# Stored weight sums and two more seven-product pairs in a down projection

## The chip, the cores and the metric

The kernel runs on one core of one Trainium2 chip. The metric is the device time of one execution in microseconds (us); lower is better. The core has a matrix engine (TensorE, PE), a vector engine (VectorE, DVE), a scalar engine (ScalarE, ACT), GpSimd (POOL), and SyncE (SP). Each runs its own instructions in order and waits on semaphores for the others. SP and POOL issue most DMAs, each on a queue of its own.

## The reference

One layer of an encoder for 256 positions of width 2048: a mixer block and a convolutional gated MLP, then a final norm. The change touches the MLP alone:

```python
def conv_ffn(x, g_norm, w_up, conv_k, conv_b, w_down):
    h = rms_norm(x, g_norm)
    up = h @ w_up                       # 256 x 2048 @ 2048 x 11008
    ...                                 # depthwise conv of width 3 over positions
    gate, val = jnp.split(up, 2, axis=-1)
    return x + (jax.nn.silu(gate) * val) @ w_down    # 256 x 5504 @ 5504 x 2048
```

The mixer block before it (an input projection, a gated branch, neighbourhood attention, an output projection) is as in the kernel before.

## The kernel before

All weights are float32. For the matrix engine each float32 operand is written as a sum of two values of a shorter format, a high part and a low part; one product then is three matmuls (a *triple*: high x high, low x high, high x low). ACT makes the high part by a copy (`whi`, L151), DVE the low part by a subtraction (`wlo`, L152). The notes call the two together the split.

Weights arrive in *pieces* by DMAs on SP into five buffers (`wraw`, `LOAD_AHEAD`). For the down projection a piece is 128 rows of `w_down` by 1024 columns, 512 KB. `begin(i)` is called ahead of the matmuls of piece i: it issues loads up to piece i + 4, splits up to piece i + 3 (four buffers each of `whi` and `wlo`), and then runs the tasks that were registered for step i with `at(i, ...)`. So the order on every engine is written out by these step numbers.

The down projection is two *groups* of 1024 columns, one after the other; each walks over the 43 blocks of 128 rows, taken two at a time as *pairs* (21 pairs and one single block). With two blocks of positions, two of rows and two of columns, a pair is a 2 x 2 by 2 x 2 block product. Done plainly it is eight triples (`plain`), twelve matmuls a piece. In the pairs listed in `DOWN_QUADS` it is done with seven products in the manner of Strassen and Winograd: the products take sums of the activations' blocks and of the weights' blocks, and the results are put together after the last such pair of a group (`ev_sums`). At the first piece of such a pair three triples are issued, at the second four.

For a seven-product pair whose first piece is step i:

- The sums of the activations (`sums` in `ev_up`) are made and split during the up projection, stored to device memory (`so`, L1010), and fetched in each group at step i - 4 by a POOL DMA (`stored`, L1157) into one of two tiles (`s0`, `s1`).
- The four sums of weight blocks (`weight_sums`, L324 to L327) are made by DVE at step i - 3 from both pieces' buffers, into the tiles `t13` and `t24`, of which there is one each.
- They are split at step i - 2 (`weight_sums_split`, L334 on ACT and L335 on DVE) into `h13`, `h24`, `l13`, `l24`, of which there are two sets (`both_rooms`).
- Of the pieces themselves only one half of the first and both halves of the second are split (`units`).

The up projection ahead of it runs over 22 groups (`g_up`) of eight pieces of `w_up`, with the convolution and the gate of one group (`conv`, `gate`) as tasks of the next one's steps. The convolution of the last groups runs in the first steps of the down projection. At step 6 of the down projection `open_fin` has POOL load two parts of the final norm's scale (`gfin`).

Of the kernel before, what the change touches and what calls it, by code (L numbers as in the profile page):

```python
# [8 lines left out]
F32 = mybir.dt.float32  # L9
# [46 lines left out]
OUT_ORDER = (tuple(range(16)), (0, 1, 6, 7, 2, 3, 10, 11, 4, 5, 8, 9, 12, 13, 14, 15))  # L56
TURN_X2 = (13, 1)
Y_GAP = 224
DOWN_PAIRS = (3, 5, 7, 9, 10, 12, 14, 16, 17, 19)
DOWN_QUADS = (DOWN_PAIRS, (2, 4, 6, 8, 9, 11, 13, 14, 16, 18))  # L60


@with_exitstack
def trunk_kernel(ctx, tc, x, x_t, vecs, w_in, ln_g, ln_b, w_st, b_s, rpb, w_branch, w_out, w_up, w_down,
                 norm_final, out):
    nc = tc.nc
    ctx.enter_context(tc.manual_schedule())

    def pool(name, side="left", bufs=1, space=None):
        kw = {} if space is None else {"space": space}  # L70
        st = ExitStack()
        p = st.enter_context(tc.tile_pool(name=name, bufs=bufs, side=side, reuse_waits="tile", **kw))
        return p, st

    def keep(name, side="left", bufs=1, space=None):
        p, st = pool(name, side, bufs, space)
        ctx.push(st)
        return p
# [22 lines left out]
    def plan_wide(src, row0, order, c0):  # L101
        first = len(pieces)
        for k in order:
            pieces.append((src, row0 + k * 128, 2, (c0, 512, 1, 0), 512))
        return first

    raw, split_t = {}, {}
    whole, units = {}, {}
    n_loaded = [0]
    n_split = [0]  # L110

    def load_to(n):
        while n_loaded[0] < min(n, len(pieces)):
            i = n_loaded[0]
            n_loaded[0] += 1
            if i in preload:
                for f in preload[i]:
                    f()
            src, r0, kn, (c0, cn, nb, cs), step = pieces[i]
            w = wpool.tile([128, 2, 512], F32, name="wraw", bufs=LOAD_AHEAD)  # L120
            ld = src.shape[-1]
            if i == 0:
                for k in range(kn):
                    nc.sync.dma_start(w[:, k, :cn], src[r0:r0 + 128, c0 + k * step:c0 + k * step + cn])
            elif nb == 1:
                nc.sync.dma_start(
                    w[:, :kn, :cn],
                    bass.AP(tensor=src.tensor, offset=src.offset + r0 * ld + c0,
                            ap=[[ld, 128], [step, kn], [1, cn]]))
            else:  # L130
                for b in range(nb):
                    nc.sync.dma_start(
                        w[:, :kn, b * cn:(b + 1) * cn],
                        bass.AP(tensor=src.tensor, offset=src.offset + r0 * ld + c0 + b * cs,
                                ap=[[ld, 128], [step, kn], [1, cn]]))
            raw[i] = w
            if i in whole:
                whole[i] = w
# [31 lines left out]
    def at(i, f):  # L170
        tasks.setdefault(i, []).append(f)
# [6 lines left out]
    def begin(i):  # L178
        cur[0] = i
        load_to(i + LOAD_AHEAD)  # L180
        if i < len(SPLIT_TO):
            run_tasks(i)
            split_to(SPLIT_TO[i])
        else:
            split_to(i + SPLIT_AHEAD + 1)
            run_tasks(i)
# [75 lines left out]

    def wide(src, row0, order, c0, acts, quads, room, done, sums=None, odd=None, stored=None, split_room=None):
        n0 = plan_wide(src, row0, order, c0)
        boxes = {}
        for n, q in enumerate(quads):
            i = n0 + 2 * q
            own = odd if odd and n % 2 else split_room or room  # L270
            whole[i] = whole[i + 1] = None
            units[i], units[i + 1] = 1, 2
            b = boxes[q] = {}
            if stored:
                b["acts"] = {}
                at(i - 4, lambda b=b, k=order[2 * q]: stored(k // 2, b["acts"]))
            else:
                b["acts"] = sums[order[2 * q]]
            at(i - 3, lambda i=i, b=b: weight_sums(i, b, room))
            at(i - 2, lambda b=b, own=own: weight_sums_split(b, own))  # L280
        return ("wide", n0, order, acts, quads, boxes, done)

# [38 lines left out]
    def weight_sums(i, box, room):  # L321
        r0, r1 = whole.pop(i), whole.pop(i + 1)
        t13, t24 = room("t13", F32), room("t24", F32)
        nc.vector.tensor_add(t13[:, 0], r0[:, 0], r0[:, 1])  # L324
        nc.vector.tensor_add(t24[:, 1], t13[:, 0], r1[:, 1])
        nc.vector.tensor_add(t13[:, 1], r0[:, 1], r1[:, 1])  # L326
        nc.vector.tensor_add(t24[:, 0], r1[:, 0], t24[:, 1])  # L327
        box["w"] = (t13, t24)

    def weight_sums_split(box, room):  # L330
        u = []
        for name, t in zip(("13", "24"), box.pop("w")):
            h, l = room("h" + name, F32R), room("l" + name, F32R)
            nc.scalar.activation(h, t, AF.Copy)  # L334
            nc.vector.tensor_sub(l, t, h.bitcast(F32))  # L335
            u.append((h, l))
        box["t"] = {1: [x[:, 0] for x in u[0]], 3: [x[:, 1] for x in u[0]],
                    2: [x[:, 1] for x in u[1]], 4: [x[:, 0] for x in u[1]]}
# [166 lines left out]
    def first_room(name, dt):  # L505
        return ypool.tile([128, 2, 512], dt, name=f"y{first_rooms.index('t13' if name == 'f' else name)}")
# [387 lines left out]
    def ev_sums(j, room):  # L894
        def done(P, i):
            x2 = rs["x2"]
            p1, p5, p6, p7 = P
            x11, x12, x21, x22 = (x2[:, t, c * 512:(c + 1) * 512] for t in range(2) for c in (j, j + 1))
            m = {}

            def first_half():
                ab, cd = room("t13", F32), room("t24", F32)
                m["v"], m["u3"], m["w"] = cd[:, 0], cd[:, 1], ab[:, 0]
                nc.scalar.activation(ab[:, 0], p1, AF.Copy)
                nc.vector.tensor_add(x11, p1, x11)
                nc.vector.tensor_sub(ab[:, 1], ab[:, 0], p6)
                nc.vector.tensor_add(m["v"], p5, ab[:, 1])
                nc.vector.tensor_add(m["u3"], p7, ab[:, 1])
                nc.vector.tensor_add(m["w"], p5, m["u3"])

            def second_half():
                nc.vector.tensor_sub(x12, x12, m["v"])
                nc.vector.tensor_add(x21, x21, m["u3"])
                nc.vector.tensor_sub(x22, x22, m["w"])

            at(i + 1, first_half)
            at(i + 2, second_half)
        return done
# [47 lines left out]
    ff = {}  # L966
# [132 lines left out]
    w_br, w_o, w_u, w_d = w_branch[0], w_out[0], w_up[0], w_down[0]  # L1099
# [6 lines left out]
    def odd_room(name, dt):  # L1106
        return s_room["odd"].tile([128, 2, 512], dt, name=name)

    first_sums = {2 * q: {} for q, _, _ in X_SUMS}
    g_v = wide(w_in2, 0, V_ORDER, V0, xt, V_QUADS, first_room, (ev_v_sums, ev_v), first_sums,  # L1110
               odd_room)
    g_va = wide(w_in2, 0, VA_ORDER, VA0, xt, VA_QUADS, first_room, (ev_va_sums, ev_va), first_sums)
    for n, (q, i, j) in enumerate(X_SUMS):
        sum_acts_at(i, j, first_sums[2 * q], lambda q=q: q,
                    lambda name, dt, i=i: first_room("s2" if name == "f" and i < 9 else name, dt), f"s{n}", True)
# [19 lines left out]
    for n, q in enumerate(GATE_PAIRS):  # L1135
        i = g_gw[0][1] - 3 + 3 * n
        sum_acts_at(i, i + 1, x_sums[2 * q], lambda q=q: x_pairs[q], sums_room, f"s{n}")
    for n, q in enumerate(OUT_PAIRS):
        i = g_o[0][1] + 3 + 3 * n
        sum_acts_at(i, i + 1, m_sums[2 * q], lambda q=q: mg["pairs"][q], sums_room, f"s{n}")  # L1140
    g_up = []
# [12 lines left out]
    def stored(pair, box):  # L1154
        n = ff["turn"] = ff.get("turn", -1) + 1
        o = down_room(f"s{n % 2}", F32R)
        nc.gpsimd.dma_start(o.bitcast(F32), ff["kept"][pair])  # L1157
        box["s"] = sums_of(o)

    def down_order(g):  # L1160
        free = [p for p in range(NF // 2) if p not in DOWN_PAIRS]
        kept = list(DOWN_PAIRS)
        pairs = [(kept if q in DOWN_QUADS[g] else free).pop(0) for q in range(NF // 2)]
        return tuple(2 * p + kk for p in pairs for kk in range(2)) + (NF - 1,)

    g_dn = [wide(w_d, 0, down_order(g), g * 1024, lambda k: ff["a"][k], DOWN_QUADS[g], down_room,
                 (ev_sums(2 * g, down_room), ev_down if g == 0 else finish), stored=stored, split_room=both_rooms) for g in range(2)]
    dram = keep("dram", space=bass.MemoryType.DRAM)
    ff["kept"] = {p: dram.tile([128, 2, 512], F32, name=f"sums{p}") for p in DOWN_PAIRS}

    preload[0] = [lambda: load_xt(0, 1)]
# [170 lines left out]
```

## Time and profile before

| | |
|---|---|
| median of 3 runs | 1307.95 us (1307.38 to 1308.11) |
| profiled execution | 1307.83 us, its span 1306.0 us |
| granted clock of TensorE, mean | 0.997 |
| PE, DVE, ACT, POOL busy | 99%, 82%, 59%, 8% of the span |
| DMA | 277.19 MB, mean 212 GB/s |
| up projection | about 590 to 1076 us |
| down projection, first matmul to last | 1076.3 to 1297.0 us |

The span is the time from the first to the last instruction of the profiled execution; the device time has a little around it. In the page, a row of 40 digits shows the busy share of each fortieth of the span in tenths. A row such as `wlo<-wraw,whi` names the tile written and the tiles read, L152 the line of the kernel. In the order of time the columns are start, duration, engine and line; in square brackets is how long the engine was idle before and what ended that. Durations of successive instructions of one engine overlap a little, so the pace is read from start to start.

### The profile page before, as it was taken

What the parts mean: (1) busy time and instruction counts of PE and PEld (TensorE: products, weight loads), DVE (VectorE), ACT (ScalarE), POOL (GpSimd) and SP (SyncE); (2) the same over time, 40 slices, a digit from 0 to 9 for tenths busy, and PEclk for the clock granted to TensorE, in tenths of its full rate; (3) what the DMA queues carried; (4) which work ended last, traced back from release to release, by engine and by line L of the source; (5) the groups of instructions that cost most, each with busy time, mean ns of one, the idle gap of its engine ahead of it and who ended that gap; (6) DMA issues with size and microseconds to landing.
All of it is one profiled execution on the core that took longest, in us unless ns stands there. A gap on an engine that the chain in (4) does not pass through costs nothing.

```text
span 1306.0 us, 19254 instructions
## 1 busy us (share of the span) xinstructions
PE 1293.6 (99%) x6712; PEld 1103.9 (85%) x6712; DVE 1072.5 (82%) x1616; ACT 776.8 (59%) x1153; POOL 104.7 (8%) x206
## 2 busy tenths in 40 slices
PE   9999999999999999999999999999999999999997
PEld 7888888888888888888888888888888888888885
DVE  7997777667689966986778878787888889999997
ACT  7766476666655644556556556565555656665563
POOL 0005405413000000000000000000000000000000
PEclk9999999999999999999999999999999999999998
DMA  9779657556556657565566566666666658876782
GB/s 351 251 243 258 191 166 214 175 171 195 177 170 204 218 182 248 202 211 163 177 195 209 182 211 198 215 194 212 191 211 199 215 161 286 288 267 227 265 290 105
DMA packets 174225, 277.19 MB, mean 212 GB/s; under 512 B 13488, under 2 KB 121904, under 8 KB 174128
## 3 DMA queue, kind: packets, MB, share of 16 engines
q1 hardware_dynamic: 165520, 252.28, 59.5%
q0 software_dynamic: 8032, 23.03, 5.5%
q8 instruction: 52, 0.85, 0.3%
q10 hardware_dynamic: 576, 0.66, 0.1%
q14 instruction: 45, 0.37, 0.1%
HBM read 266.48 MB, written 7.34 MB: 210 GB/s over the span
## 4 chain that ended last, share of the span: by engine, by line
PE 96%; DVE 1%; ACT 1%; DMA 1%; issue 0%; SPq 0%; ACTq 0%; DVEq 0%
PE bank L203 31%; PE bank L207 16%; PE bank L291 11%; PE bank L289 11%; PE bank L290 11%; PE bank L231 5%; PE bank L233 4%; PE bank L232 4%; DMA wraw<-in_w_in_dram 1%; PE bank L756 1%; PE bank L806 0%; DVE wlo L152 0%; PE bank L622 0%; PE bank L796 0%; PE bank L887 0%
## 5 line engine op out<-in xcount | busy, mean ns | idle before, releaser
L152 DVE TENSOR_TENSOR wlo<-wraw,whi 128x1024 fp32r<-128x1024 f32 (+1 forms) x472 | 546.0, 1170 | 182.5 <-ACT whi L151 100.4
L151 ACT ACTIVATE whi<-wraw 128x1024 fp32r<-128x1024 f32 (+1 forms) x472 | 470.3, 1010 | 218.4 <-PE bank L290 85.1
L203 PE MATMUL bank<-h,whi 128*128 128x512 f32 x1760 | 425.5, 392 | 0.0
L203 PEld LDWEIGHTS bank<-h,whi 128*128 128x128 f32 x1760 | 322.1, 188 | 61.7
L207 PEld LDWEIGHTS bank<-h,wlo 128*128 128x128 f32 x1760 | 225.9, 191 | 8.8
L207 PE MATMUL bank<-h,wlo 128*128 128x256 f32 x1760 | 228.6, 283 | 0.0
L985 ACT ACTIVATE tc<-ta,ck 128x256 f32<-128x256 f32 x86 | 47.1, 594 | 117.1 <-DVE ta L983 117.1
L291 PE MATMUL bank<-wlo,a 128*128 128x512 f32 x224 | 87.3, 390 | 0.0
L290 PE MATMUL bank<-whi,a 128*128 128x512 f32 x224 | 87.2, 389 | 0.0
L289 PE MATMUL bank<-whi,a 128*128 128x512 f32 x224 | 87.1, 389 | 0.0
L289 PE MATMUL bank<-whi,h 128*128 128x512 f32 x210 | 82.4, 393 | 0.6 <-ACT h L495 0.6
L291 PE MATMUL bank<-wlo,h 128*128 128x512 f32 x210 | 81.9, 390 | 0.7 <-DVE wlo L152 0.7
L290 PE MATMUL bank<-whi,h 128*128 128x512 f32 x210 | 81.8, 390 | 0.8 <-DVE h L496 0.8
L334 ACT ACTIVATE h<-h 128x1024 fp32r<-128x1024 f32 x40 | 40.2, 1053 | 33.7 <-DVE h L326 33.7
L988 DVE SCALAR_TENSOR_TENSOR tc<-ta,ck,tc 128x255 f32<-128x255 f32 x86 | 41.4, 481 | 14.4 <-ACT tc L985 14.4
L231 PE MATMUL bank<-whi,y 128*128 128x512 f32 x128 | 50.5, 394 | 0.0
L231 PE MATMUL bank<-whi,h 128*128 128x512 f32 x128 | 50.4, 394 | 0.0
L233 PE MATMUL bank<-wlo,h 128*128 128x512 f32 x128 | 49.9, 390 | 0.0
L233 PE MATMUL bank<-wlo,y 128*128 128x512 f32 x128 | 49.9, 390 | 0.0
L232 PE MATMUL bank<-whi,y 128*128 128x512 f32 x128 | 49.8, 389 | 0.0
L232 PE MATMUL bank<-whi,h 128*128 128x512 f32 x128 | 49.8, 389 | 0.0
L291 PEld LDWEIGHTS bank<-wlo,a 128*128 128x128 f32 x224 | 42.0, 188 | 9.1 <-DVE wlo L152 0.3
(284 smaller groups left out, 1786.0 us busy)
## 6 DMA issues: line engine op xcount, KB each, us to landing
wraw<-in_w_up_dram SPq DMA_DIRECT2D x336, 256.0 KB, 3.2
wraw<-in_w_in_dram SPq DMA_DIRECT2D x111, 512.0 KB, 4.5
wraw<-in_w_down_dram SPq DMA_DIRECT2D x86, 512.0 KB, 5.4
wraw<-in_w_in_dram SPq DMA_DIRECT2D x66, 256.0 KB, 3.3
wraw<-in_w_branch_dram SPq DMA_DIRECT2D x32, 512.0 KB, 4.6
wraw<-in_w_out_dram SPq DMA_DIRECT2D x32, 512.0 KB, 4.0
h<-sums POOLq DMA_DIRECT2D x20, 512.0 KB, 7.0
sums<-so POOLq DMA_DIRECT2D x10, 512.0 KB, 5.4
```

Of the source, the lines that this page charges most:

```text
L151: nc.scalar.activation(h[:, k, :m], w[:, k, :m], AF.Copy)
L152: nc.vector.tensor_sub(l[:, k, :m], w[:, k, :m], h[:, k, :m].bitcast(F32))
L203: nc.tensor.matmul(p, h[:, k - k0, b * 128:(b + 1) * 128], acts(k), start=k == 0, stop=k == nk - 1)
L207: nc.tensor.matmul(p[:, :T], l[:, k - k0, b * 128:(b + 1) * 128], acts(k)[:, 0, :], start=False, stop=False)
L231: nc.tensor.matmul(p, xh, h[:, kk, :m], start=st, stop=False)
L232: nc.tensor.matmul(p, xl, h[:, kk, :m], start=False, stop=False)
L233: nc.tensor.matmul(p, xh, l[:, kk, :m], start=False, stop=sp)
L289: nc.tensor.matmul(p, xh, h, start=st, stop=False)
L290: nc.tensor.matmul(p, xl, h, start=False, stop=False)
L291: nc.tensor.matmul(p, xh, l, start=False, stop=sp)
L985: nc.scalar.activation(v, u, AF.Identity, scale=ck[:, 1, ch:ch + 1], bias=ck[:, 3, ch:ch + 1])
L988: nc.vector.scalar_tensor_tensor(v[:, 1:], u[:, :T - 1], ck[:, 0, ch:ch + 1], v[:, 1:], op0=OP.mult, op1=OP.add)
```

## The change

There are now twelve seven-product pairs in each group instead of ten, and they stand in adjacent twos: 3 and 4, 6 and 7, and so on in the first group, 2 and 3, 5 and 6 and so on in the second. For four of the twelve in each group (`DOWN_KEPT`, the first of each of the middle four twos) the four weight sums are made ahead:

- During the up projection, in groups 3, 5, ... 17, `sums_ahead` loads a pair's weights (1 MB) on POOL's queue at a group's first step, makes the four sums on DVE at its steps 4 and 5, and stores them to device memory (1 MB) on POOL's queue.
- In the down projection `stored_weights` fetches them with two POOL DMAs of 512 KB into `t13` and `t24` at step i - 6. `weight_sums` is left out for these pairs; `weight_sums_split` at step i - 2 is as before.
- The first piece of such a pair is loaded by half, since only its first 512 columns are needed (`halved`).
- Two more pairs' activation sums are made and stored.

```diff
-DOWN_PAIRS = (3, 5, 7, 9, 10, 12, 14, 16, 17, 19)
-DOWN_QUADS = (DOWN_PAIRS, (2, 4, 6, 8, 9, 11, 13, 14, 16, 18))
+DOWN_PAIRS = (3, 4, 6, 7, 9, 10, 12, 13, 15, 16, 18, 19)
+DOWN_QUADS = (DOWN_PAIRS, (2, 3, 5, 6, 8, 9, 11, 12, 14, 15, 17, 18))
+DOWN_KEPT = ((6, 9, 12, 15), (5, 8, 11, 14))
...
             src, r0, kn, (c0, cn, nb, cs), step = pieces[i]
+            if i in halved:
+                kn = 1
...
-            whole[i] = whole[i + 1] = None
             units[i], units[i + 1] = 1, 2
+            if q in kept:
+                halved.add(i)
+            else:
+                whole[i] = whole[i + 1] = None
...
-            at(i - 3, lambda i=i, b=b: weight_sums(i, b, room))
+            if q in kept:
+                at(i - 6, lambda b=b, k=order[2 * q]: stored_weights(c0, k // 2, b, room))
+            else:
+                at(i - 3, lambda i=i, b=b: weight_sums(i, b, room))
             at(i - 2, lambda b=b, own=own: weight_sums_split(b, own))
...
+    def stored_weights(c0, pair, box, room):
+        box["w"] = room("t13", F32), room("t24", F32)
+        for n, t in enumerate(box["w"]):
+            nc.gpsimd.dma_start(t, ff["weights"][c0, pair][:, 2 * n:2 * n + 2])
+
+    def sums_ahead(src, c0, pair, i):
+        box = {}
+
+        def load():
+            w = box["w"] = ff["more"].tile([128, 4, 512], F32, name="tw")
+            ld = src.shape[-1]
+            nc.gpsimd.dma_start(w, bass.AP(tensor=src.tensor, offset=src.offset + 256 * pair * ld + c0,
+                                           ap=[[ld, 128], [128 * ld, 2], [512, 2], [1, 512]]))
+
+        def first_two():
+            w = box["w"]
+            nc.vector.tensor_add(w[:, 0], w[:, 0], w[:, 1])
+            nc.vector.tensor_add(w[:, 1], w[:, 1], w[:, 3])
+
+        def last_two():
+            w = box["w"]
+            nc.vector.tensor_add(w[:, 3], w[:, 0], w[:, 3])
+            nc.vector.tensor_add(w[:, 2], w[:, 2], w[:, 3])
+            nc.gpsimd.dma_start(ff["weights"][c0, pair], w)
+
+        at(i, load)
+        at(i + 4, first_two)
+        at(i + 5, last_two)
...
+    jobs = [(g * 1024, down_order(g)[2 * q] // 2) for g in range(2) for q in DOWN_KEPT[g]]
+    ff["weights"] = {job: dram.tile([128, 4, 512], F32, name=f"weights{n}") for n, job in enumerate(jobs)}
+    for n, job in enumerate(jobs):
+        sums_ahead(w_d, *job, g_up[3 + 2 * n][1])
```

More of the change, by code (lines that the diff above doesn't have):

```diff
@@ L107, in trunk_kernel @@
     raw, split_t = {}, {}
-    whole, units = {}, {}
+    whole, units, halved = {}, {}, set()
     n_loaded = [0]
@@ L260, in run_group, with wide @@
             done(ps, b)
-    def wide(src, row0, order, c0, acts, quads, room, done, sums=None, odd=None, stored=None, split_room=None):
+    def wide(src, row0, order, c0, acts, quads, room, done, sums=None, odd=None, stored=None, split_room=None, kept=()):
         n0 = plan_wide(src, row0, order, c0)
@@ L1166, in trunk_kernel @@
     g_dn = [wide(w_d, 0, down_order(g), g * 1024, lambda k: ff["a"][k], DOWN_QUADS[g], down_room,
-                 (ev_sums(2 * g, down_room), ev_down if g == 0 else finish), stored=stored, split_room=both_rooms) for g in range(2)]
+                 (ev_sums(2 * g, down_room), ev_down if g == 0 else finish), stored=stored, split_room=both_rooms, kept=DOWN_KEPT[g]) for g in range(2)]
     dram = keep("dram", space=bass.MemoryType.DRAM)
+    jobs = [(g * 1024, down_order(g)[2 * q] // 2) for g in range(2) for q in DOWN_KEPT[g]]
+    ff["weights"] = {job: dram.tile([128, 4, 512], F32, name=f"weights{n}") for n, job in enumerate(jobs)}
+    for n, job in enumerate(jobs):
+        sums_ahead(w_d, *job, g_up[3 + 2 * n][1])
     ff["kept"] = {p: dram.tile([128, 2, 512], F32, name=f"sums{p}") for p in DOWN_PAIRS}
```

## The prediction

> **What bounds the kernel now.** I read the page from the top: engine shares, the 40 slices, the chain; then windows of the stage that the change touches, and inside it the order of time on each engine.
>
> ```profile
> PE 1293.6 (99%) x6712; PEld 1103.9 (85%) x6712; DVE 1072.5 (82%) x1616; ACT 776.8 (59%) x1153; POOL 104.7 (8%) x206
> ...
> DVE  7997777667689966986778878787888889999997
> ...
> DMA  9779657556556657565566566666666658876782
> ...
> PE 96%; DVE 1%; ACT 1%; DMA 1%; issue 0%; SPq 0%; ACTq 0%; DVEq 0%
> ```
>
> TensorE (PE) is busy for 99% and makes 96% of the chain that ends last: the time falls only with the number of products, and rises with every wait that reaches PE. In the last seven slices, the down projection, VectorE (DVE) stands at 9 and the DMA engines at 7 to 8, both higher than before. The windows say it in numbers (first the up projection, then the two groups of the down projection); the columns are busy time of each engine, the granted clock, the DMA share and GB/s:
>
> ```profile
> core 0: us, PE busy (x) PEld busy (x) DVE busy (x) ACT busy (x) POOL busy (x), PEclk, DMA share, GB/s
> 700.00:1000.00 300.00, 300.00 (x1727) 265.20 (x1726) 244.37 (x418) 176.56 (x280) 4.32 (x8) 1.00 0.65 203
> 1080.00:1180.00 100.00, 100.00 (x443) 82.77 (x442) 95.99 (x116) 60.23 (x69) 6.39 (x12) 1.00 0.81 279
> 1200.00:1275.00 75.00, 75.00 (x332) 62.10 (x332) 73.81 (x90) 45.19 (x50) 5.31 (x10) 1.00 0.78 274
> ```
>
> DVE has 19% free in the up projection (244.4 of 300) and 2 to 4% in the down projection. PE is never short there: its one wait for DVE in the whole stage is this, and the loads are held back by buffers that DVE has yet to free, not by the memory:
>
> ```profile
> SPq L126 <- DVE wlo L152: 106.2, 58, 4.8
> ...
> PEld bank L291 <- DVE wlo L152: 0.3, 1, 0.3
> ```
>
> **What the change takes off PE.** A pair done plainly is 8 triples of matmuls, a seven-product pair 7. The groups go from ten such pairs to twelve: 4 triples less, 12 matmuls. Starts of matmuls in order of time (first of the stage, two a triple apart, last):
>
> ```profile
> 1076.31 0.39 PE L289 MATMUL bank<-whi,a 128*128 128x512 f32 x1
> ...
> 1109.83 0.39 PE L289 MATMUL bank<-whi,a 128*128 128x512 f32 x1
> ...
> 1110.51 0.39 PE L289 MATMUL bank<-whi,a 128*128 128x512 f32 x1
> ...
> 1296.63 0.39 PE L291 MATMUL bank<-wlo,a 128*128 128x512 f32 x1
> ```
>
> A triple takes 0.68 us, a matmul 0.227 (the 0.39 is one matmul's pipelined length). The stage has 2 x (10 x 21 + 11 x 24 + 12) = 972 matmuls; (1296.63 - 1076.31) / 971 = 0.2269, so it holds almost no gap. Twelve fewer: **-2.7 us**, 0.21%. That is the whole possible gain. About 0.2% (2.6 us) is what a measurement of this kernel can tell from no change.
>
> **DVE's account.** Its order in time around step 6 of the first group:
>
> ```profile
> 1092.00 1.22 DVE L152 TENSOR_TENSOR wlo<-wraw,whi 128x1024 fp32r<-128x1024 f32 x1
> 1093.13 2.35 DVE L335 TENSOR_TENSOR h<-h,h 128x1024 fp32r<-128x1024 f32 x2
> 1095.40 2.95 DVE L152 TENSOR_TENSOR wlo<-wraw,whi 128x1024 fp32r<-128x1024 f32 x3
> 1098.28 0.68 DVE L324 TENSOR_TENSOR h<-wraw 128x512 f32<-128x512 f32 x1
> ...
> 1100.81 1.22 DVE L152 TENSOR_TENSOR wlo<-wraw,whi 128x1024 fp32r<-128x1024 f32 x1
> 1101.94 2.36 DVE L335 TENSOR_TENSOR h<-h,h 128x1024 fp32r<-128x1024 f32 x2
> ```
>
> From start to start: a full split 1.13, the two splits of a pair's sums 2.27, the three of 1095.40 (two full, one half) 2.88, so a half split 0.62, and the four weight sums 1098.28 to 1100.81, 2.53. A seven-product pair costs DVE 0.62 + 1.13 + 2.53 + 2.27 = 6.55 us against 21 x 0.227 = 4.8 on PE; a plain pair 2.26 against 5.4. A kept pair drops the 2.53. Over the stage 16 pairs instead of 20 need sums (-10.1), four more are split (4 x (2.27 - 0.51) = +7.0): DVE loses 3.1 us, PE 2.7. On the mean nothing gets tighter; what changes is the order.
>
> *First twos.* Pairs 3 and 4 of the first group are both unkept and now adjacent, where pair 4 was plain. DVE then has at 1095.40, instead of three splits: half split 0.62, sums 2.53, full split 1.13 (and 0.09 to its end): 1099.77. PE needs that split at the third matmul of pair 4's second triple, matmul 72 + 21 + 5 of the stage: 1076.31 + 98 x 0.2269 = 1098.55. **+1.2 us**; below zero is excluded, since nothing earlier on DVE moves, and if DVE starts the stage 1.2 us earlier it is nothing. The other group begins with no convolution tail on DVE; I put nothing there.
>
> *Stored sums.* A kept pair's sums come by two 512 KB transfers on GpSimd's queue (POOL), into the same two tiles that the pair before has just used: they are issued only when DVE has split that pair. ACT and DVE then wait for them in order, with the splits of the following pieces queued behind. The trace has no such transfer; the nearest are the activation sums on the same queue, as large:
>
> ```profile
> 1075.82 0.53 POOL L1157 DMA_DIRECT2D h<-sums  x1 [10.19 <-PE bank L207]
> 1076.77 0.53 POOL L1157 DMA_DIRECT2D h<-sums  x1 [0.41 <-PE bank L203]
> 1089.15 0.54 POOL L1297 DMA_DIRECT2D gfin<-in_norm_final_dram  x1 [11.85 <-DVE tc L996]
> 1092.38 0.54 POOL L1297 DMA_DIRECT2D gfin<-in_norm_final_dram  x1 [2.69 <-DVE a L481]
> ```
> ```profile
> DMA to landing us min/median/max: 4.6/7.0/9.4
> ```
> ```profile
> q0 software_dynamic: 8032, 23.03, 5.5%
> ```
>
> Issues can follow 0.95 us apart; landing takes 4.6 to 9.4, median 7.0. In the first group pair 4's two splits end at 1100.9 and 1102.0 (1099.68 + 1.22, + 1.13), so the sums of pair 6 are issued at 1101.0 and 1102.1. Behind them on POOL stand the two loads of the final scale (1103.05, 1104.0), which today leave by 1092.38, and then pair 6's activation sums, 1104.95, which today have the queue to themselves. PE asks for these at matmul 144: 1076.31 + 32.67 + 1.2 = 1110.2. They land at 1109.6, 1112.0 or 1114.4, so PE waits 0, 1.8 or 4.2. I take a quarter of the way from median to longest, because 1.5 MB lies ahead of them: **+2.3 us**.
>
> *The chain from kept to kept.* In the middle of a group every three pairs (kept, unkept, plain) take PE 66 x 0.2269 = 15.0 us. The sums of the next kept pair cannot be issued before the unkept pair between is split, and that is behind the last kept one on DVE. The ring: second transfer issued 1.13 after the first; landing 7.0; and behind the first transfer's data, q0's price being 5.5% x 1306 us x 0.524 / 23.03 MB = 1.6 us for 512 KB alone, twice that if SP's loads take every other turn, so 0.5 to 2.1 later (I take 0.5, since SP's loads have pauses): 8.6. Then ACT's copy,
>
> ```profile
> 1100.32 2.01 ACT L334 ACTIVATE h<-h 128x1024 fp32r<-128x1024 f32 x2 [3.77 <-DVE h L326]
> ```
>
> 1.0 each, and DVE's 1.13 + 0.62 + 2.53 + 1.13 + 1.22: 16.3 us with two handovers. That is 1.3 us more than PE's 15.0, per link, three links in each group. With the shortest landing the ring is 13.9 and costs nothing; with the longest and 2.1 it is 20.3, 5.3 per link. Against it stands a lead: pair 6's last split ends at 1102.1 + 7.5 + 1.0 + 1.2 = 1111.8 and PE needs it at matmul 155, 1076.31 + 35.2 + 1.2 + 2.3 = 1115.0: 3.2 us in the first group, 0.9 in the second, which has no 2.3 before it. So 3.9 - 3.2 = 0.7 and 3.9 - 0.9 = 3.0: **+3.7 us**.
>
> A figure for this stands in the Trainium skill, "DMA: Bandwidth & Descriptors", section "Anatomy of one DMA — SWDGE (gpsimd) path": about 2.0 us plus bytes at 436 GB/s, my estimate 3.2 us for 512 KB. By it the ring would close in 12 us and the activation sums come in time, leaving -1.5 us; the trace disagrees, its shortest is 4.6.
>
> *Made ahead.* Eight times in the up projection: a 1 MB load, four adds (2.53 us in two steps), a 1 MB store; and two more pairs' activation sums. Free time hides it: DVE's idle time ahead of its splits alone was, in the 300 us,
>
> ```profile
> L152 DVE TENSOR_TENSOR wlo<-wraw,whi 128x1024 fp32r<-128x1024 f32 x108 | 132.1, 1223 | 42.4 <-PE bank L207 36.3 <-ACT whi L151 6.1
> ```
>
> 42.4 us against some 17 us added to it, and 16 MB more in eight double groups is 47 GB/s on 203 at a share of 0.65. Zero; without that cover it would be up to 20 us. The 8 halved loads on SP (256 KB less each) cost nothing.
>
> Sum: -2.7 + 1.2 + 2.3 + 3.7 = +4.5. The profiled execution took 1307.83 us (span 1306.0 and 1.8 around it), 0.1 under the median 1307.95: **1312.4 us** for the median.
>
> **Rivals.** *Quick transfers.* The sums land in under 6 us, both waits on them vanish, the first twos stay: -2.7 + 1.2 = -1.5, 1306.4 us. For it: the shortest row, 4.6. Against it: the median of 7.0, with less traffic (279 GB/s) than there will be (332, worked out below). The Trainium skill's fit in "DMA: Bandwidth & Descriptors" would give this case.
>
> *All covered.* DVE also begins the stage early enough: -2.7, 1305.2 us, the one way to faster. Against it: the quoted order, 1.2 us late with nothing before it removed.
>
> *The DMA engines bind.* Three pairs in the middle move 6 x 512 - 256 KB of pieces, 1 MB of activation sums and 1 MB of weight sums, 4.98 MB in 15.0 us: 332 GB/s. Today's 279 at a share of 0.81 makes 344 at a full share, so 332 fits on paper with 4% to spare. If the engines sustain only 300, the three pairs take 16.6 us, 1.6 more, eight times: +13 + 1.2 - 2.7 = +11.5, 1319.5 us; it decides below 332. The Trainium skill, same page, section "Specifications", gives 358 GB/s for a core from HBM; by that it would not bind, and the sum stands.
>
> **How the numbers follow.** Forecast 0.56, its own range +2 to +9 (1310 to 1317); quick transfers 0.22; all covered 0.09; DMA bound 0.13. Faster by over 0.2%: 0.09. Within: the quick case and a twelfth of the forecast, 0.27. Slower: 0.64. The range leaves out the covered case and the upper part of the bound case: 1306.4 to 1318.5.
>
> **What would show it.** PE's waits in the stage should name wlo at the first group's step 8, h<-sums at step 12, and wlo or h<-sums every 15 us after; the weight-sum transfers should land 7 us or more after issue, POOL's final-scale loads after 1102; the up projection should show PE without a gap. It is wrong if the stored sums land in under 6 us, if step 8 has no wait, or if gaps appear before 1076.

## Result, and the profile after

The changed kernel takes 1328.02 us (median of 5 runs, 1324.84 to 1332.1), the kernel before 1307.95 beside it: a ratio of 1.0155, 95% interval 1.0133 to 1.0177. It is slower by 20 us; the forecast was slower by 4.5, and the range ended at 1318.5. The profiled execution took 1332.1 us (span 1330.2), 24.3 more than the profiled one of before. The page of after, the rows that answer to those of before:

```profile
PE 1301.6 (98%) x6700; PEld 1105.4 (83%) x6700; DVE 1092.3 (82%) x1650; ACT 780.2 (59%) x1163; POOL 126.9 (10%) x244
...
PEclk9999999999999999999999999999999998999898
...
q0 software_dynamic: 14528, 51.34, 11.7%
...
PE 85%; issue 6%; DMA 5%; DVE 3%; ACT 1%; POOL 0%; SPq 0%; ACTq 0%; DVEq 0%; POOLq 0%
```

PE issues twelve matmuls fewer, as meant, and POOL's queue (q0) moves 51 MB instead of 23. DVE still has 82%: no engine took over as the busiest. But PE's part of the chain fell from 96% to 85%, with DMA and "issue" in its place, and in the last seven slices the granted clock shows an 8 three times. The windows, the three of before and then two short ones around one gap (the columns as before):

```profile
700.00:1000.00 300.00, 300.00 (x1727) 265.19 (x1726) 261.98 (x452) 174.47 (x279) 13.67 (x23) 1.00 0.78 252
1080.00:1180.00 100.00, 91.92 (x392) 74.66 (x392) 82.14 (x99) 55.19 (x66) 10.61 (x20) 0.97 0.81 289
1200.00:1275.00 75.00, 69.63 (x290) 55.49 (x289) 61.64 (x73) 42.06 (x52) 9.53 (x18) 0.95 0.74 253
1110.00:1118.00 8.00, 2.16 (x8) 1.49 (x7) 5.78 (x8) 3.67 (x5) 0.00 (x0) 0.83 0.94 368
1118.00:1123.00 5.00, 5.00 (x15) 3.87 (x15) 5.00 (x5) 2.75 (x3) 1.30 (x3) 0.59 0.81 253
```

The up projection is untouched: PE is busy for all of its 300 us, with 17.6 us more of DVE and 49 GB/s more of traffic beside it. The down projection lost it all. There DVE is *less* busy than before (82.1 of 100, 61.6 of 75) and PE is short by 7 to 8%: work arrives late, no engine is full. Starts of matmuls run from 1077.09 to 1320.83, 243.7 us for 960 of them; at 0.2267 us from start to start, the pace without a gap, 959 steps are 217.4, so 26.3 us are lost where before it was 0.2. The waits in the down projection, us in total, times, longest, show on what:

```profile
POOL h L342 <- DVE h L373: 129.3, 16, 25.7
...
PE bank L298 <- DMA h<-sums: 13.5, 4, 5.8
...
PE bank L300 <- DVE wlo L155: 2.5, 3, 1.2
```

PE waits mostly for activation sums (`h<-sums`), and POOL stands 129 us, always ahead of a weight-sum transfer, until DVE has split the pair before. The order of time on POOL (start, us, what, idle before and what ended it) shows how the two belong together:

```profile
1101.97 0.53 POOL L342 DMA_DIRECT2D h<-weights  x1 [23.88 <-DVE h L373]
1103.11 0.53 POOL L342 DMA_DIRECT2D h<-weights  x1 [0.60 <-DVE h L373]
1103.78 1.08 POOL L1339 DMA_DIRECT2D gfin<-in_norm_final_dram  x2
1104.85 1.06 POOL L1195 DMA_DIRECT2D h<-sums  x2
1119.98 0.53 POOL L342 DMA_DIRECT2D h<-weights  x1 [14.06 <-DVE h L373]
...
1136.92 0.53 POOL L342 DMA_DIRECT2D h<-weights  x1 [8.60 <-DVE h L373]
1138.04 0.53 POOL L342 DMA_DIRECT2D h<-weights  x1 [0.59 <-DVE h L373]
1138.56 0.53 POOL L1195 DMA_DIRECT2D h<-sums  x1
```

At the third of these pairs the activation sums leave right behind the weight sums, without a pause: they had been waiting in POOL's program behind an instruction that waited for DVE. The weight sums themselves leave every 18.0, 16.9 and 17.2 us in the first group, 17.4, 18.6 and 18.7 in the second, where PE's three pairs take 15.0. Landing of weight sums, then of activation sums (7.0 before):

```profile
DMA to landing us min/median/max: 4.7/6.8/9.5
```
```profile
DMA to landing us min/median/max: 5.8/9.1/13.6
```

And PE around step 8 and step 12:

```profile
1099.29 0.39 PE L299 MATMUL bank<-whi,a 128*128 128x512 f32 x1
1100.60 0.50 PE L300 MATMUL bank<-wlo,a 128*128 128x512 f32 x1 [0.92 <-DVE wlo L155]
...
1110.93 0.39 PE L300 MATMUL bank<-wlo,a 128*128 128x512 f32 x1
1117.16 0.79 PE L298 MATMUL bank<-whi,h 128*128 128x512 f32 x1 [5.84 <-DMA h<-sums]
1117.76 0.63 PE L299 MATMUL bank<-whi,h 128*128 128x512 f32 x1
1118.18 0.63 PE L300 MATMUL bank<-wlo,h 128*128 128x512 f32 x1
```

The second gap is 6.2 us from start to start, the largest of all. What follows it was not foreseen: the next matmuls start 0.43 us apart instead of 0.227, eleven of them, while the granted clock of the window is 0.59. It cost another 2.4 us. The other three waits for activation sums come much later, one in the first group and two in the second:

```profile
1165.94 0.50 PE L298 MATMUL bank<-whi,h 128*128 128x512 f32 x1 [1.32 <-DMA h<-sums]
...
1245.89 0.79 PE L298 MATMUL bank<-whi,h 128*128 128x512 f32 x1 [3.84 <-DMA h<-sums]
...
1281.92 0.50 PE L298 MATMUL bank<-whi,h 128*128 128x512 f32 x1 [2.49 <-DMA h<-sums]
```

Each is the third product of a kept pair, the first use of its activation sums.

### The profile page after: what moved, and what is told of

Its sections match the earlier page's. It is cut to its first block, busy times and chain, and to the rows that moved or that the text cites. A ratio compares the mean times of both kernels' runs of the same rounds, so it can differ in the third digit from the quotient of the medians.

```text
span 1330.2 us, 19356 instructions
## 1 busy us (share of the span) xinstructions
PE 1301.6 (98%) x6700; PEld 1105.4 (83%) x6700; DVE 1092.3 (82%) x1650; ACT 780.2 (59%) x1163; POOL 126.9 (10%) x244
## 4 chain that ended last, share of the span: by engine, by line
PE 85%; issue 6%; DMA 5%; DVE 3%; ACT 1%; POOL 0%; SPq 0%; ACTq 0%; DVEq 0%; POOLq 0%
PE bank L206 30%; PE bank L210 16%; PE bank L300 8%; PE bank L298 8%; PE bank L299 8%; PE bank L234 4%; PE bank L236 4%; PE bank L235 4%; DMA h<-sums 4%; DVE wlo L155 1%; DMA wraw<-in_w_in_dram 1%; PE bank L794 1%; DMA h<-weights 0%; ACT whi L154 0%; PE bank L844 0%
## 5 line engine op out<-in xcount | busy, mean ns | idle before, releaser
L154 ACT ACTIVATE whi<-wraw 128x1024 fp32r<-128x1024 f32 (+1 forms) x472 | 465.1, 1005 | 190.5 <-PE bank L299 69.9
L298 PE MATMUL bank<-whi,h 128*128 128x512 f32 x214 | 85.3, 398 | 14.2 <-DMA h<-sums 13.5
L372 ACT ACTIVATE h<-h 128x1024 fp32r<-128x1024 f32 x48 | 49.1, 1054 | 70.6 <-DMA h<-weights 40.4
L299 PE MATMUL bank<-whi,h 128*128 128x512 f32 x214 | 84.0, 393 | 0.8 <-DVE h L534 0.8
L300 PE MATMUL bank<-wlo,a 128*128 128x512 f32 x200 | 78.5, 393 | 2.7 <-DVE wlo L155 2.5
L373 DVE TENSOR_TENSOR h<-h,h 128x1024 fp32r<-128x1024 f32 x48 | 57.2, 1220 | 28.9 <-ACT h L372 28.9
L299 PE MATMUL bank<-whi,a 128*128 128x512 f32 x200 | 77.9, 389 | 0.0
L298 PE MATMUL bank<-whi,a 128*128 128x512 f32 x200 | 77.8, 389 | 0.0
L298 PEld LDWEIGHTS bank<-whi,h 128*128 128x128 f32 x214 | 40.5, 189 | 25.5 <-DMA h<-sums 15.9
L234 PE MATMUL bank<-whi,h 128*128 128x512 f32 x128 | 50.4, 394 | 0.0
```

The source lines that it names most:

```text
L154: nc.scalar.activation(h[:, k, :m], w[:, k, :m], AF.Copy)
L234: nc.tensor.matmul(p, xh, h[:, kk, :m], start=st, stop=False)
L298: nc.tensor.matmul(p, xh, h, start=st, stop=False)
L299: nc.tensor.matmul(p, xl, h, start=False, stop=False)
L300: nc.tensor.matmul(p, xh, l, start=False, stop=sp)
```

## The experiments

Three theories at first. **A, order:** the activation sums come late because they stand behind the weight sums in POOL's program. **B, load:** the DMA engines have too much to move. **C, twos:** the adjacent twos overload DVE. A fourth came after the first four runs: **D, the ring:** a weight-sum transfer waits for the single tiles `t13` and `t24`, which are free only when the pair before is split; it is the ring of the prediction's chain. Each run is compared with the kernel before on the same chip (1307.95 to 1308.28). Line numbers shift by one to three between kernels.

**Which half of the change.** All twelve pairs with live sums, nothing stored; and the old ten pairs, four of each group stored:

```diff
-DOWN_KEPT = ((6, 9, 12, 15), (5, 8, 11, 14))
+DOWN_KEPT = ((), ())
```

> All twelve pairs' weight sums are made by DVE again (none stored), the adjacent twos stay. Theory A (the stored weight sums hold up the activation sums on POOL's queue): no transfer of weight sums is left, so PE waits for no h<-sums; DVE needs 6.55 + 6.55 + 2.26 = 15.4 us for three pairs against PE's 15.0, so some 3 to 5 us of waits on wlo: 1309 to 1312 us. Theory B (the DMA engines are full): nearly the same, 1309 to 1312. Theory C (the adjacent twos overload DVE, the stored sums matter little): as slow as the changed kernel or slower, 1325 us or more.

```diff
-DOWN_PAIRS = (3, 4, 6, 7, 9, 10, 12, 13, 15, 16, 18, 19)
-DOWN_QUADS = (DOWN_PAIRS, (2, 3, 5, 6, 8, 9, 11, 12, 14, 15, 17, 18))
-DOWN_KEPT = ((6, 9, 12, 15), (5, 8, 11, 14))
+DOWN_PAIRS = (3, 5, 7, 9, 10, 12, 14, 16, 17, 19)
+DOWN_QUADS = (DOWN_PAIRS, (2, 4, 6, 8, 9, 11, 13, 14, 16, 18))
+DOWN_KEPT = ((7, 9, 12, 16), (6, 8, 11, 13))
```

> The ten pairs of the kernel before at their old places, with four in each group (7, 9, 12, 16 and 6, 8, 11, 13) stored ahead. PE has as many products as before. Theory A: the activation sums of a kept pair are asked for one plain pair later than in the twos, so they land in time or nearly: 1308 to 1311 us. Theory B: around a kept pair the traffic is the same 332 GB/s (3.41 MB in 10.3 us), so waits of 1 to 3 us at each of eight: 1315 to 1330 us. Theory C: no twos beyond those of before and less work for DVE, 1308 us.

Live sums: 1316.13 us, ratio 1.006 (1.0043 to 1.0076), more than expected; PE waits for `wlo` alone. Stored with the old pairs: 1313.12, 1.0034 (1.0021 to 1.0048), between what A and B had expected, with a single wait on `h<-sums`, 3.5 us, at a kept pair of the second group, and 1.8 us of slow matmuls behind it. Either half costs by itself: with all sums live the twos (C) cost 8 us. Storing sums, meant to relieve DVE, makes the twelve pairs dearer by 12 us.

**POOL's order.** The activation sums on ACT's queue; and, in another kernel, the final scale loaded later:

```diff
-        nc.gpsimd.dma_start(o.bitcast(F32), ff["kept"][pair])
+        nc.scalar.dma_start(o.bitcast(F32), ff["kept"][pair])
```

> The changed kernel with the activation sums fetched by DMAs on ACT's queue; the weight sums stay on POOL's. The bytes are the same. Theory A: the activation sums no longer stand behind the weight sums, PE waits for none of them: 1306 to 1310 us, with the wait of 1.1 us at step 8 left. Theory B: the landing stays at 9 us and the waits stay: 1322 us or more. Theory C: 1320 us or more, with waits on wlo.

```diff
-    at(g_dn[0][1] + 6, open_fin)
+    at(g_dn[0][1] + 30, open_fin)
```

> The changed kernel with the two loads of the final scale moved from step 6 to step 30 of the first group. Theory A: the wait at step 12 shrinks from 6.0 us by 2 to 3 us (two issues of 0.5 us and 512 KB less ahead of the sums); if it falls under 2 us the 2.6 us of slow matmuls behind it go as well: 1321 to 1325 us. Theory B: the same bytes move elsewhere, 1327 us. Theory C: 1327 us.

On ACT's queue the time is 1324.18, ratio 1.0128 (1.0113 to 1.0143). The waits of PE and the transfers of that kernel:

```profile
PE bank L300 <- DVE wlo L155: 12.0, 8, 2.0
```
```profile
h<-sums ACTq DMA_DIRECT2D x24, 512.0 KB, 6.1
h<-weights POOLq DMA_DIRECT2D x16, 512.0 KB, 6.1
```

So the activation sums land in 6.1 us instead of 9.1 (medians of all 24), the ones of the first kept pair leave 5.6 us sooner (1099.29 against 1104.85), and PE waits for none of them. Only 4 us came back, far less than A had expected, since another wait was right behind it: the `wlo` rows, every three pairs. The weight sums still leave at a pitch of 16.3, 16.7 and 16.3 us in the first group and 15.2, 18.6 and 17.2 in the second. The place is read from the order of time on PE:

```profile
1115.04 0.39 PE L299 MATMUL bank<-whi,a 128*128 128x512 f32 x1
1116.50 0.50 PE L300 MATMUL bank<-wlo,a 128*128 128x512 f32 x1 [1.07 <-DVE wlo L155]
```

This is the sixth matmul of pair 7, the unkept pair behind the kept one. Six waits stand at this place in the two groups, 10.0 us together. On DVE that split starts at 1115.23, behind the kept pair's two splits, a half split and four weight sums.

With the scale late the wait at step 12 fell from 6.0 to 3.7 us, as theory A has it, but the median was 1328.87 (1.0153, 1.0132 to 1.0174). Runs of each kernel spread over some 7 us, more than the effect; as to the total this one is inconclusive.

**The single tiles.** This tests D. The stored sums go into the low-part tiles `l13` and `l24`, of which there are two sets, and are split in place, so that they need not wait for `t13` and `t24`. The bytes stay. Once with the activation sums on ACT's queue, once on POOL's as in the changed kernel:

```diff
-        box["w"] = room("t13", F32), room("t24", F32)
+        box["l"] = both_rooms("l13", F32R), both_rooms("l24", F32R)
+        box["w"] = [t.bitcast(F32) for t in box["l"]]
...
-            h, l = room("h" + name, F32R), room("l" + name, F32R)
+            h, l = room("h" + name, F32R), box["l"][k] if "l" in box else room("l" + name, F32R)
```

> The run with the activation sums on ACT's queue, and now the stored weight sums land in the tiles l13 and l24, of which there are two sets, and are split in place; so their fetch no longer waits for DVE to have split the pair before in t13 and t24, but for PE to have used the pair two before. The bytes are the same. Theory D (a ring: fetch, split, next pair's sums, its split, next fetch, 16 to 17 us against PE's 15.0): the six waits on wlo of 1.2 to 2.1 us at every third pair go, the first (1.1) and last (2.2) stay, and half of the small ones: 1310 to 1314 us. Theory B (the DMA engines are full): the transfers land as late, 1321 us or more.

> The changed kernel, activation sums on POOL's queue as in it, with the stored weight sums landing in l13 and l24 as in the run beside it. Theory A with D: the fetch now waits on POOL for PE, and the activation sums still stand behind 1 MB on POOL's queue: waits on h<-sums of 2 to 4 us at the kept pairs, 1316 to 1326 us. Theory D alone: as the run beside it, 1310 to 1314 us. Theory B: 1325 us or more.

On POOL's queue: 1311.23 us, ratio 1.0024 (1.0014 to 1.0033), 17 us of the 20 given back by the choice of tiles. On ACT's: 1313.43, 1.0037 (1.0023 to 1.005). PE's waits in the kernel on POOL's queue, its transfers, and when the first two sets of weight sums leave:

```profile
PE bank L300 <- DVE wlo L155: 2.3, 3, 1.2
PE bank L298 <- DMA h<-sums: 1.9, 3, 1.0
```
```profile
h<-sums POOLq DMA_DIRECT2D x24, 512.0 KB, 8.5
h<-weights POOLq DMA_DIRECT2D x16, 512.0 KB, 7.7
```
```profile
1097.30 0.53 POOL L343 DMA_DIRECT2D h<-weights  x1 [19.37 <-PE bank L300]
...
1114.45 0.53 POOL L343 DMA_DIRECT2D h<-weights  x1 [9.94 <-DVE h L336]
```

The transfers take about as long to land as in the changed kernel (8.5 against 9.1, 7.7 against 6.8); they leave sooner, at a pitch of 17.2, 15.0, 15.0 and 16.3, 15.0, 15.5 us. The first leaves at 1097.30 instead of 1101.97. That settles D for the bulk of the loss: the ring through the single tiles. POOL's order matters little once the ring is open.

**What is left, by DVE's order.** Twelve fewer matmuls should give -2.7, and 3 us were still lost. Three kernels with the new tiles, the first from the one on ACT's queue and the other two from the one on POOL's, for the idea that DVE's load and the first twos hold it: a single pair first in group one; that and five kept pairs instead of four; five kept pairs alone. All load the final scale late. The edit of the first; the other two add a fifth kept pair (17 or 18) to each group, made ahead from group 1 on:

```diff
-DOWN_QUADS = (DOWN_PAIRS, (2, 3, 5, 6, 8, 9, 11, 12, 14, 15, 17, 18))
-DOWN_KEPT = ((6, 9, 12, 15), (5, 8, 11, 14))
+DOWN_QUADS = ((3, 5, 6, 8, 9, 11, 12, 14, 15, 17, 18, 20), (2, 3, 5, 6, 8, 9, 11, 12, 14, 15, 17, 18))
+DOWN_KEPT = ((5, 8, 11, 14), (5, 8, 11, 14))
```

> The run with ACT's queue and the tiles of their own, with the first group's seven-product pairs at 3, 5, 6, 8, 9, 11, 12, 14, 15, 17, 18, 20 (kept: 5, 8, 11, 14), so that no two unkept ones stand together at its start, and the final scale loaded from step 30 on. Theory D: the wait of 1.1 us at step 8 goes: 1 to 2 us below the first run of this call. Theory B: 1320 us or more.

> The run on POOL's queue with the tiles of their own, with five kept pairs in each group instead of four (5, 8, 11, 14, 17), the first group's pairs shifted to 3, 5, 6, 8, 9, 11, 12, 14, 15, 17, 18, 20, the final scale loaded from step 30 on, and ten sets of sums made in up-projection groups 1, 3, ... 19. DVE has 2 x 2.53 us less to do in the down projection. Theory D (only the ring and DVE's order mattered): no wait at step 8, fewer on wlo at the end of the groups: 1306 to 1309 us. Theory B (bytes): two more sets of 768 KB, waits on h<-sums or h<-weights: 1312 us or more.

> The same with the pairs at the changed kernel's places (kept: 6, 9, 12, 15, 18 and 5, 8, 11, 14, 17). Theory D: the wait of 1.1 us at step 8 stays, the waits at the groups' ends (1.3 us in the second) go: 1307 to 1310 us. Theory B: 1312 us or more.

They gave 1315.2 (ratio 1.005, 1.0033 to 1.0067), 1313.46 (1.0046, 1.0033 to 1.0059) and 1315.38 (1.0056, 1.0044 to 1.0068). None beat 1311.23. With the single start the wait at step 8 is gone, and PE waits elsewhere; with the fifth kept pair DVE has less to do and it helps nothing. The idea missed. The fifth pair also adds bytes, and both kernels with it came out where theory B had put them, at 1312 or more.

**What is left, by bytes.** Half of each weight-sum transfer, with zeros in place of the other half, so that part of the computation is left out; the transfer twice; two spare transfers on ACT's queue; the same two on POOL's:

```diff
-            nc.gpsimd.dma_start(t, ff["weights"][c0, pair][:, 2 * n:2 * n + 2])
+            nc.gpsimd.dma_start(t[:, 0:1], ff["weights"][c0, pair][:, 2 * n:2 * n + 1])
+            nc.gpsimd.memset(t[:, 1:2], 0.0)
```

> As the run with the stored sums in tiles of their own on POOL's queue (1311.2 us), but each of the two weight-sum transfers fetches only one of its two sums, 256 KB instead of 512 KB; POOL fills the other half with zeros. Those products come out of zeros: part of the computation is left out. What is left over the kernel before, 3 us, is then either traffic or order. Traffic: 4 MB less in the stage, 0.5 MB less per kept pair, so POOL's queue clears earlier; the three waits on h<-sums (1.9 us) go, and the time falls to 1308 to 1310. Order on DVE (first twos, splits behind one another): the transfers only have to come in time, which they do already; 1310.5 to 1312.

> As the run with the stored sums in tiles of their own on POOL's queue (1311.2 us), but each of the two weight-sum transfers is issued twice, the same bytes into the same tile: 8 MB more in the stage, 2 MB instead of 1 MB per kept pair. Traffic: the three pairs around a kept one move 6.0 MB in 15.0 us, 400 GB/s where the windows of the kernel before put a full share at 344; they take 17.4 us, 2.4 us more, eight times: 1325 to 1332. Queue only: the engines keep up, but the activation sums stand behind 2 MB instead of 1 MB, some 1.5 to 3 us later each: 1315 to 1322. Order on DVE: neither matters while the rooms are free, 1311 to 1313.

```diff
+        for n in range(2):
+            nc.scalar.dma_start(ff["spare"][c0, pair][:, 2 * n:2 * n + 2], ff["weights"][c0, pair][:, 2 * n:2 * n + 2])
```

> As the run with the stored sums in tiles of their own (1311.2 us), with two more transfers of 512 KB per kept pair, on ACT's queue, from the stored sums in device memory to spare device memory that nobody reads or waits for. If the load on the DMA engines is what stored bytes cost: halving them gave back 4.3 us for 4 MB, so 8 MB more cost at least 8.6, and more where the share nears one (middle of a group: 303 + some 70 GB/s, against 344 worked out for a full share); 1320 to 1330. If only the place on POOL's queue counts: the activation sums keep their place, 1311 to 1314.

> The same two spare transfers per kept pair, on POOL's queue, right behind the weight sums and ahead of the activation sums. Load: as with ACT's queue, 1320 to 1330. Place on the queue: the activation sums land some 3 us later (512 KB alone cost POOL's queue 1.6 us) at each of eight kept pairs, where PE already waits for them at three; 8 x 2 to 3, and slow matmuls behind the longer waits: 1327 to 1340.

Half: 1306.95 us (ratio 0.9993, 0.9984 to 1.0002). PE's one wait in the stage is the first twos:

```profile
PE bank L300 <- DVE wlo L155: 0.9, 1, 0.9
```
```profile
h<-sums POOLq DMA_DIRECT2D x24, 512.0 KB, 7.5
...
h<-weights POOLq DMA_DIRECT2D x16, 256.0 KB, 5.9
```

Everything lands 1 to 2 us sooner and the remaining waits are gone, although DVE does the same work; order on DVE alone is out as their cause. Halving also halves what stands ahead of the activation sums on POOL's queue, so this run alone does not tell load from place. Twice: 1400.4 (1.0707, 1.0692 to 1.0721), which tells nothing of load:

```profile
POOL h L344 <- DMA h<-weights: 84.5, 11, 9.3
```

The second copy into a tile waits on POOL until the first has landed, and all of POOL's program behind it; I had overlooked that wait. So the bytes were added again where nobody waits for them. On ACT's queue: 1337.81 (1.0235, 1.0212 to 1.0257), 26.6 us more than without. A window of the first group, PE's waits, and the transfers:

```profile
1085.00:1195.00 110.00, 99.78 (x417) 80.57 (x416) 88.96 (x103) 58.94 (x67) 11.64 (x22) 0.95 0.85 309
```
```profile
PE bank L298 <- DMA h<-sums: 23.4, 8, 4.4
```
```profile
h<-sums POOLq DMA_DIRECT2D x24, 512.0 KB, 12.5
...
h<-weights POOLq DMA_DIRECT2D x16, 512.0 KB, 10.0
spare<-weights ACTq DMA_DIRECT2D x16, 512.0 KB, 10.8
```

Nothing was put ahead of the activation sums on their queue, and they land 4 us later. On POOL's queue: 1346.97 (1.0302, 1.0288 to 1.0316), 9.2 more than on ACT's, the price of the place. Both came out some 7 us above what was expected. So added bytes cost by load first and by place second. That the last 3 us are load (theory B) fits all these runs, but how they divide into load and place is not shown. A fixed ceiling near 300 GB/s it is not: the kernel with the stored sums in `l13` and `l24`, on POOL's queue, moved 335 GB/s at a share of 0.92 from 1215 to 1260 us, and the changed kernel 368 at 0.94 in the 8 us shown above.

**Old pairs, own tiles.** The second kernel of all, with the edit of the tiles:

> The old ten pairs per group with four of each kept (1313.1 us before), now with the stored sums in tiles of their own. If its one 3.5 us wait on the activation sums and the slow matmuls after it came from the single tiles that delay the transfers, they go and the time is that of the kernel before, 1307.5 to 1309.0, since it has the same 972 matmuls and no adjacent twos beyond those of before. If stored sums cost by their bytes whatever the tiles, it stays at 1311 to 1314.

1308.02 us (0.9997, 0.9989 to 1.0006): no difference from the kernel before, and no wait of PE over 0.25 us in the stage. The 5 us that storing cost with these pairs were the single tiles too. In the first group (1085 to 1195 us) DVE is now busy for 95.75 of 110 us, 105.30 before: the time that stored sums were to buy is there, and nothing uses it. No kernel that computes everything was measurably faster than the one before.

## Why the prediction was wrong in size

The sign came as forecast, and so did the kinds of wait; the size did not, and one cost was not in the sum at all. By the steps, in the profiled execution:

- **Twelve matmuls, -2.7, and the up projection at nothing: right.** The half-bytes kernel shows the first almost alone: its matmuls run for 218.9 us against 220.3 before, which is -2.7, one wait of 1.1 and trifles.
- **First twos, +1.2: right.** 1.08 measured.
- **Step 12, +2.3: 6.0.** The weight sums left at 1101.97 and 1103.11, 1 us behind the forecast, but the activation sums at 1104.85, as forecast (1104.95). PE had them at 1117.16, 12.3 us after issue; I had taken a quarter of the way from 7.0 to 9.4. The worst row of before was no bound for a transfer with 1.5 MB ahead of it.
- **Chain from kept to kept, +3.7: the step that failed.** In the profile all waits over 0.25 us apart from step 8 and step 12 come to 10.6, of which 8.1 are for activation sums at three later kept pairs (1.5, 4.0 and 2.65) and the rest for `wlo`. The ring was 16.3 us on paper; where it is alone (sums on ACT's queue) the first group has 16.3 to 16.7 and the second 17.0 on the mean, so its length was about right. Two things were not. The lead was measured at the wrong consumer: at the kept pair's own last split (3.2 and 0.9 us to spare). DVE still has a half split, four sums and a full split to do before PE's next need, the sixth matmul of the unkept pair. With the prediction's own figures that is 1111.8 + 0.62 + 2.53 + 1.13 + 0.09 = 1116.2, needed at matmul 164: 1076.31 + 37.2 + 1.2 + 2.3 = 1117.0, a lead of 0.8. In the second group the 0.9 becomes -1.5 likewise, and 3.9 - 0.8 + 3.9 + 1.5 gives +8.5; the six waits at that place with the sums on ACT's queue are 10.0. Next, the activation sums were put behind the weight sums once, at step 12, though the same program order holds at every kept pair, where they took 8.0 to 11.3 us to land; they, and not the splits, are what PE mostly waited for. With both in place the pitch was 16.9 to 18.7 us. The kernel with the other tiles gave 17 us back, at step 12 and in the chain: that shows the single tiles to be the main cause of both.
- **Not in the sum: the clock, put at nothing without a reason.** After three of the gaps matmuls ran at about half pace: 2.4 + 2.9 + 1.8 = 7.1 us.

Together -2.7 + 1.1 + 6.0 + 10.6 + 7.1 = 22.1; some 1.5 of small waits and a stage that began 0.8 later make up, less the 0.2 that before lost, the 24.2 by which the span grew.

Of the rivals, *quick transfers* (1306.4) is what half the bytes gave, 1306.95. It lost on its condition: sums in under 6 us. *The DMA engines bind* came nearest by its number (1319.5) but not as the main cause: the same bytes in other tiles cost 3 us and not 20. *All covered* fell with the first twos. Of what would show it, `wlo` at step 8, `h<-sums` at step 12, the final scale after 1102 and an up projection without a gap came. Two signs did not come as written: after step 12 the first group has one more such wait, 49 us later, and not one every 15 us (PE was already 8 us late there, and the pitch of the ring, 18.0, 16.9 and 17.2 against 15.0, used that up first); and the weight sums landed in 6.8 us by the median, not in 7 or more.

## What to carry to other kernels

A transfer that replaces computing needs a tile that is free early; here that was 17 us of 20, and the bytes at most the rest: before fetching something ahead, ask who must let go of its destination, and close that ring with the *next* consumer on every in-order engine, not with the step that the transfer feeds. What stands behind a waiting DMA instruction in a queue's program waits with it, each time round. And where PE is the bound, price a wait by its length plus what the clock takes after it.

## What the runs showed of the hardware

The clock: in the down projections of all these kernels, after a stand-still of PE of 2.40 us or more from start to start, 6 to 14 matmuls follow at about 0.43 us instead of 0.227, 1.4 to 3.0 us in all (once, after 3.49 us, there were none); after 2.33 us or less there was no such run of them. The traces have the granted clock at 0.5 for 3.41 us or a multiple of it each time; in the changed kernel it is 6.83 us twice and 3.41 once. A case from each side, from the kernel with the sums on ACT's queue and the one with all sums live:

```profile
1240.29 0.39 PE L299 MATMUL bank<-whi,a 128*128 128x512 f32 x1
1242.62 0.50 PE L300 MATMUL bank<-wlo,a 128*128 128x512 f32 x1 [1.94 <-DVE wlo L155]
1242.95 0.40 PE L298 MATMUL bank<-whi,h 128*128 128x512 f32 x1
1243.19 0.40 PE L299 MATMUL bank<-whi,h 128*128 128x512 f32 x1
```
```profile
1293.89 0.39 PE L299 MATMUL bank<-whi,a 128*128 128x512 f32 x1
1296.33 0.52 PE L300 MATMUL bank<-wlo,a 128*128 128x512 f32 x1 [2.05 <-DVE wlo L155]
1296.66 0.61 PE L298 MATMUL bank<-whi,a 128*128 128x512 f32 x1
1297.08 0.63 PE L299 MATMUL bank<-whi,a 128*128 128x512 f32 x1
```

After the first start the matmuls are 0.24 us apart in the one, 0.42 in the other. The Trainium skill, "TensorE: Matmul & The Clock Gate", section "What's actually happening", has half the clock after an idle window of about 3.4 us; these runs agree on the half, and see it from 2.4 us on.

Landing, the median of the 24 transfers of activation sums, 512 KB each: 5.5 us on POOL's queue with no stored weight sums (the kernel with all sums live), 9.1 with 1 MB of them at each kept pair on the same queue (the changed kernel), and 12.5 with 1 MB more at each kept pair on ACT's queue (8.5 without, in the same tiles).
